# Input products of a decoder trunk as block products of seven multiplications, with attention and pooling put between them

## The chip, the cores and the metric

The kernel runs on one core of one Trainium2 chip. The metric is the device time of the whole program in microseconds (us). Three runs of the kernel before gave a median of 2831.74 us (2831.07 to 2831.84). The profile shows one execution, of 2828.03 us; its span from the first to the last instruction is 2826.3 us. The engines are named as in the profile: PE is TensorE, DVE is VectorE, ACT is ScalarE, POOL is GpSimd, SP is SyncE; PE, DVE, ACT and POOL compute, SP and POOL issue DMAs here.

## What is computed

One pre-norm block on x of 2048 positions by 1024 channels. The normalised input goes through one input projection into queries, keys and values of 12 heads, the pooling input (768 channels) and two gates (1024 channels each). Attention runs over three head groups with windows dilated by 1, 4 and 16 positions; their outputs are combined with weights from their softmax denominators. Pooling takes trailing means over 2, 4, 8 and 16 positions. Both are projected, gated, added, projected again and added to x; a squared-ReLU MLP (1024 to 4096 to 1024) and a last norm follow.

```python
HEAD_DIM = 64
ATT_GROUPS = ((128, 1), (512, 4), (2048, 16))
HEADS_PER_GROUP = 4
POOL_WINDOWS = (2, 4, 8, 16)
D_FF = 4 * D_MODEL
...
    s = jnp.einsum('znqhd,znkhd->znhqk', qb, kb) * (Dh ** -0.5)
    ...
    s = jnp.where(valid[None, :, None], s + bias[None, None], -jnp.inf)
    lse = jax.nn.logsumexp(s, axis=-1)
    p = jnp.exp(s - lse[..., None])
    o = jnp.einsum('znhqk,znkhd->znqhd', p, vb).reshape(Z, Lp, H, Dh)[:, :L]
...
    wts = jax.nn.softmax(jnp.stack(lses, axis=0), axis=0)
    merged = jnp.sum(wts[..., None] * outs, axis=0)
```

## The kernel before

Activations lie with channels on the partitions and positions along the row, in blocks of 128 by 512; a chunk `c` is 512 positions, a half `hf` 1024. Every large product is done to float32 accuracy with three matmuls of rounded parts: an operand is cast to a high part (ACT), the difference to it is the low part (DVE), and high by high, high by low and low by high are summed in PSUM.

The program is one list of stages; a scheduler puts each engine's instructions in order, and they run in that order. The stages are:

- fold: the pooling projection is multiplied by the per-group map into `w_pzg_d` (L213 to L234).
- a1 (the first `for c in range(NCH)`): per chunk, `gained_x` loads x times a gain without the norm, six products give q, k, v of group 2, and the sum of squares becomes `rstd`, which is applied where the results leave PSUM.
- a2: per chunk, six products for the pooling input, the pooling sums (L372), and one block of `attn_g2` after four of the six.
- a3: per chunk, `norm_x`, then q, k, v of groups 1 and 0, `attn_block` for each of four blocks per group (four heads at a time: scores `s` L307, bias L311, maximum L314, exponential L316, transposes `t` L321, copy L323, output `o` L329, copy L331), and the combination of the three groups (L458 to L502), whose weights go to DRAM (`wts_d`) and come back spread over the partitions (`wb`).
- gates(0), merge(0), gates(1), residual(0), merge(1), mlp_in(0), residual(1), mlp_in(1). Gates, residual and mlp_in go through `stage`: a pair of 128-row weight tiles against a half of the input is a 2 by 2 block product done with seven multiplications (`ORDER1`) instead of eight. Two pairs run side by side; each of the seven steps is 12 matmuls of 512 columns per pair. The blocks of the input that all pairs share (`mB11` to `mT4`) are made once per stage.
- the second MLP product, also with seven multiplications, and the last norm.

Only the stages from gates on use seven multiplications; in a1 to a3 each product has its full number of matmuls: 1728 of 512 columns and 1152 of 256 columns (the values, computed with positions on the partitions).

## Time and profile before

| | |
|---|---|
| median of three runs | 2831.74 us |
| profiled execution, and its span | 2828.03 us, 2826.3 us |
| PE busy | 2643.4 us (94%) |
| DVE busy | 1849.3 us (65%) |
| ACT busy | 1337.5 us (47%) |
| POOL busy | 369.6 us (13%) |
| mean granted clock of TensorE | 0.967 |

Busy shares are means over stages with different limits. The table by stretches in the rows further down has one line for each stage: 0 to 33.5 us fold, to 175 a1, to 356 a2, to 757 a3 with products, to 798.5 the attention of the last chunk, to 840.3 the combination of the last chunk, to 1007 gates(0), to 1094.6 merge(0), to 1251 gates(1), to 1338 residual(0), to 1433.3 merge(1), to 2160 mlp_in(0), residual(1), mlp_in(1). A PE that is busy is not PE at its peak, since the ends of matmuls are modelled.

### The profile page before, as it was taken

The page shows a single profiled execution, that of the slowest core. Times are in us where ns is not written, and L with a number is a line of the kernel's source. Part 1 is how long each engine was busy: PE and PEld are TensorE (multiplying, and loading weights), DVE is VectorE, ACT ScalarE, POOL GpSimd, SP SyncE. Part 2 cuts the span into 40 slices and gives each one's busy share as a digit, 9 for nine tenths or more (in the row PEclk, how much of TensorE's full clock was granted, in tenths as well). Part 3 has the DMA queues.
Part 4 walks back from the last instruction along what each step waited for, and adds up shares of the span by engine and source line. Part 5 has one row for each costly group of instructions (what it writes and reads, how often), then busy time and mean ns, then how long its engine had stood idle before and what let it go on. Part 6 is the DMA issues. An engine that isn't in the chain of part 4 may idle for free.

```text
span 2826.3 us, 37148 instructions
## 1 busy us (share of the span) xinstructions
PE 2643.4 (94%) x12966; PEld 2170.3 (77%) x12966; DVE 1849.3 (65%) x2908; ACT 1337.5 (47%) x2472; POOL 369.6 (13%) x581
## 2 busy tenths in 40 slices
...
GB/s 262 75 108 171 167 195 142 151 93 99 79 73 164 117 257 186 111 217 251 231 224 180 161 174 257 212 199 194 189 183 231 257 146 188 229 236 112 137 101 131
DMA packets 213469, 486.67 MB, mean 172 GB/s; under 512 B 37312, under 2 KB 44480, under 8 KB 213152
## 3 DMA queue, kind: packets, MB, share of 16 engines
...
q8 instruction: 102, 1.67, 0.2%
q14 instruction: 87, 0.71, 0.1%
...
## 4 chain that ended last, share of the span: by engine, by line
PE 51%; issue 27%; DMA 10%; DVE 6%; POOL 4%; ACT 2%; SPq 0%; POOLq 0%; DVEq 0%; ACTq 0%
PE z L535 6%; PE z L536 6%; PE z L534 6%; PE z_c_b L534 2%; PE z_c_b L535 2%; PE z_c_b L536 2%; DMA wb<-wts_d 2%; PE mm_v L275 2%; POOL hid_d L734 1%; DMA x<-hid_d 1%; PE z_g_b L535 1%; PE z_g_b L536 1%; PE z_g_b L534 1%; PE mm L127 1%; PE mm L125 1%
## 5 line engine op out<-in xcount | busy, mean ns | idle before, releaser
L528 DVE TENSOR_TENSOR wl_S<-r_S,wh_S 128x512 fp32r<-128x512 f32 x128 | 88.7, 693 | 123.8 <-ACT wh_S L527 123.8
L527 ACT CAST wh_S<-r_S 128x512 fp32r<-128x512 f32 x128 | 79.7, 623 | 176.5 <-PE z L535 154.0
L535 PE MATMUL z<-xl_T,wh_S 128*128 128x512 f32 x384 | 149.6, 390 | 2.8 <-DVE xl_T L528 2.8
L528 DVE TENSOR_TENSOR wl_c_S<-s_c,wh_c_S 128x512 fp32r<-128x512 f32 x128 | 87.0, 690 | 95.5 <-ACT wh_c_S L527 95.3
L536 PE MATMUL z<-xh_T,wl_S 128*128 128x512 f32 x384 | 149.4, 389 | 0.0
L316 ACT ACTIVATE sb_g<-sb_g,negm 128x256 f32<-128x256 f32 (+1 forms) x192 | 86.2, 451 | 119.6 <-DVE negm L314 119.6
L534 PE MATMUL z<-xh_T,wh_S 128*128 128x512 f32 x384 | 138.7, 389 | 0.0
L527 ACT CAST wh_c_S<-s_c 128x512 fp32r<-128x512 f32 x128 | 77.0, 616 | 79.2 <-PE z_c_c L535 43.1
L527 ACT CAST wh_A<-r_A 128x512 fp32r<-128x512 f32 x96 | 59.5, 620 | 104.8 <-PE z L535 63.3
L528 DVE TENSOR_TENSOR wl_A<-r_A,wh_A 128x512 fp32r<-128x512 f32 x96 | 66.1, 690 | 64.8 <-ACT wh_A L527 64.1
L535 PE MATMUL z<-xl_B,wh_A 128*128 128x512 f32 x256 | 102.0, 399 | 1.5 <-DVE xl_B L528 1.5
L126 PE MATMUL mm_a<-xl_a,hi_a 128*128 128x512 f32 x256 | 102.2, 400 | 0.0
L125 PE MATMUL mm_a<-xh_a,hi_a 128*128 128x512 f32 x256 | 100.6, 400 | 1.4 <-ACT qk L410 1.4
L534 PE MATMUL z<-xh_B,wh_A 128*128 128x512 f32 x256 | 95.0, 404 | 7.1 <-ACT xh_B L527 6.6
L127 PE MATMUL mm_a<-xh_a,lo_a 128*128 128x512 f32 x256 | 101.5, 397 | 0.0
L536 PE MATMUL z<-xh_B,wl_A 128*128 128x512 f32 x256 | 99.3, 396 | 0.0
L527 ACT CAST wh_c_A<-r_c 128x512 fp32r<-128x512 f32 x96 | 59.5, 619 | 72.7 <-PE z_c_c L535 28.0
L817 POOL TENSOR_TENSOR y<-y,frs 128x256 f32<-128x256 f32 x4 | 3.2, 811 | 656.9 <-ACT fsq L802 649.3
L535 PEld LDWEIGHTS z<-xl_T,wh_S 128*128 128x128 f32 x384 | 72.1, 188 | 18.6 <-DVE xl_T L528 3.7
L527 ACT CAST wh_g_S<-s_g 128x512 fp32r<-128x512 f32 x64 | 39.4, 620 | 98.8 <-DVE s_g L601 36.0
L528 DVE TENSOR_TENSOR wl_c_A<-r_c,wh_c_A 128x512 fp32r<-128x512 f32 x96 | 65.9, 686 | 29.3 <-ACT wh_c_A L527 29.3
L536 PEld LDWEIGHTS z<-xh_T,wl_S 128*128 128x128 f32 x384 | 72.1, 188 | 14.9
(502 smaller groups left out, 8670.6 us busy)
## 6 DMA issues: line engine op xcount, KB each, us to landing
x<-hid_d SPq DMA_DIRECT2D x160, 256.0 KB, 4.5
...
r_S<-w2s_d SPq DMA_DIRECT2D x128, 256.0 KB, 2.6
x_a<-in_xt SPq DMA_DIRECT2D x96, 256.0 KB, 3.9
r_A<-in_w SPq DMA_DIRECT2D x96, 256.0 KB, 3.5
...
```

What stands on the lines that cost most here:

```text
L125: nc.tensor.matmul(ps, lh, rh, start=(i == 0), stop=False)
L126: nc.tensor.matmul(ps, lh, rl, start=False, stop=False)
L127: nc.tensor.matmul(ps, ll, rh, start=False, stop=(i == n - 1))
L275: nc.tensor.matmul(pv[t][:, :256], a, b, start=(k == 0 and n == 0), stop=(k == KD - 1 and n == 2))
L316: nc.scalar.activation(s[:, h, :W], s[:, h, :W], AF.Exp, bias=negm[:, col + h:col + h + 1], accum_out=l[:, col + h:col + h + 1])
L527: nc.scalar.copy(hi, src)
L528: nc.vector.tensor_sub(lo, src, hi.bitcast(F32))
L534: nc.tensor.matmul(ps, lh, rh, start=start and i == 0, stop=False, skip_group_check=True)
L535: nc.tensor.matmul(ps, lh, rl, start=False, stop=False, skip_group_check=True)
L536: nc.tensor.matmul(ps, ll, rh, start=False, stop=stop and i == n - 1, skip_group_check=True)
L734: nc.gpsimd.dma_start(hid_d[hf][i][j], t)
L817: nc.gpsimd.tensor_mul(y, y, rs)
```

## The change

All products of the normalised input now go through `stage`, one call per half, with 20 pairs: per head group two pairs of q and k and one pair of v, three pairs of the pooling input, eight pairs of gates. Groups go in the order 1, 0, 2 in half 0 and 2, 1, 0 in half 1. The input blocks come from `normed_x` and `combine`: both chunks of the half are loaded, their sums of squares made, and x normalised before the blocks are formed. The results go to DRAM (`qk_d`, `v_d`, `pz_d`, `sg_d`) with the positions of a group's dilation put together; values are transposed by PE in `v_pair` first.

Attention is done in units of two heads (`attention`), 96 of them, and pooling in `pooling`, both called from `hook(j)` after the two pairs of group `j`: five units (half 0) or eight (half 1) after each group from the second on, pooling after groups 6, 7 and 8. After group 8 of half 0 the hook prepares the input of half 1; after group 8 of half 1 it makes the weights of the three head groups for all positions at once (`group_weights`). The combination itself moves into `merge`, and so does the sigmoid of the gates.

In this part PSUM has three banks `b` and two `c` for products, and single banks `s0`, `s1` (scores) and `t`, which the transposes, the output of a unit, the transposed values and the sums of squares share; afterwards four `b` and four `c`. `WB` goes from 5 to 4 and `ZB` from 11 to 10. The stages after it now run as merge(0), merge(1), residual(0), residual(1), mlp_in(0), mlp_in(1). Per half, the input products are 20 pairs of 7 steps of 12 matmuls of 512 columns, 3360 in all. The 96 transposes for the values are new. The second MLP product is unchanged.

```diff
-        for c in range(NCH):
-            cs = slice(c * C, (c + 1) * C)
-            ssq = a1.tile([P, C], F32, name=f"ssq{c}", tag="ssq", bufs=2)
-            u = gained_x(c, f"a1_{c}", ssq, a1)
...
-                mm3_chunk(pqk[i], wqk[i], u)
...
-        for c in range(NCH):
-            u = gained_x(c, f"a2_{c}")
-            for n in range(6):
-                w = split_load(w_pzg_d[n], D, f"wz{c}_{n}", lo_on=nc.gpsimd)
...
-    ORDER1 = ("A11 B11 b", "S1 T1 c", "S2 T2 b", "S4 B22 c", "S3 T3 b", "A12 B21 a", "A22 T4 b")
-    RAWB, SB, WB, ZB = 4, 5, 5, 11
+    ORDER1 = ("A11 B11 b", "S1 T1 c", "S2 T2 b", "S4 B22 c", "S3 T3 b", "A12 B21 c", "A22 T4 b")
+    RAWB, SB, WB, ZB = 4, 5, 4, 10
...
+        for t in range(2):
+            for k in range(KD):
+                tag = {(0, 0): "tt", (1, 0): "hx", (1, 1): "h22", (0, 1): "zz"}[t, k // KH]
+                x = load(k, t, tag)
+                if tag != "zz":
+                    got[k, t] = x
+                if k == 0:
...
+                else:
+                    sq = wtile(f"xsq_{hf}_{k}_{t}")
+                    nc.scalar.square(sq, x)
+                    nc.vector.tensor_add(ssq[t], ssq[t], sq)
+            ps = psd.tile([P, C], F32, name=f"xst_{hf}_{t}", tag="t")
+            ssq_to_rstd(wp, ps, ssq[t], ssq[t], f"x{hf}_{t}", ("zz",) * 3, ZB)
...
+        def piece(k, t, tag):
+            x = got.get((k, t))
+            if x is None:
+                x = load(k, t, tag)
+            nc.vector.scalar_tensor_tensor(x, x, g_mix[:, k:k + 1], ssq[t], op0=ALU.mult, op1=ALU.mult)
...
+                for key, _, scale, onto, fin in js:
+                    wh, wl = split(wp, w[key][a], f"{key}_{a}", "w", WB)
+                    first = n in (0, 1, 5)
                     if first:
-                        bank[j, bk] = ps_c(f"{kj}_{bk}")
-                    ps = bank[j, bk]
+                        bank[key, bk] = bank_of(bk, f"{key}_{bk}{n}")
+                    ps = bank[key, bk]
                     mm_acc(ps, [(wh[:, k * P:(k + 1) * P], wl[:, k * P:(k + 1) * P], *m[b][k])
...
+                        fin(1, 0, ps, None)
+            if hook:
+                hook(j0 // 2)
...
+        def fin(row, t, ps, mid):
+            c = 2 * hf + t
+            o = wtile(f"zq_{key}_{row}_{t}") if mid is None or d > 1 else mid
+            if d > 1:
+                total(o.rearrange("p (r i) -> p r i", r=d), ps.rearrange("p (i r) -> p r i", r=d),
...
+            nc.gpsimd.dma_start(qk_d[g][2 * i + row, :, :, c * C // d:(c + 1) * C // d],
+                                o.rearrange("p (r i) -> p r i", r=d))
...
+        def fin(row, t, ps, mid):
+            z = finished(key, row, t, ps, mid)
+            pt = psd.tile([P, C], F32, name=f"vt_{key}_{row}_{t}", tag="t")
...
+                nc.tensor.transpose(pt[:, b * P:(b + 1) * P], z[:, b * P:(b + 1) * P], ident)
...
+            nc.scalar.copy(vt, pt)
+            nc.gpsimd.dma_start(v_d[g][at(hf, t), row * P:(row + 1) * P].rearrange("(b p) f -> p b f", p=P),
...
+        z = temp(f"pz_{key}", "hx", TW)
+        nc.sync.dma_start(z, pz_d[n, :, c * C:c * C + TW])
...
+            nc.vector.tensor_add(s[rows, 2 * w - 1:], prev[rows, 2 * w - 1:], prev[rows, w - 1:H0 + C - w])
...
+        nc.gpsimd.dma_start(p_d[c, n], pf)
...
+        qk = temp(f"qk_{key}", "hx", 3 * P)
+        q, k = qk[:, :P], qk[:, P:P + W]
+        nc.sync.dma_start(q, qk_d[g][hp, :, r, own])
+        nc.sync.dma_start(k, qk_d[g][2 + hp, :, r, ks])
+        vo = temp(f"vo_{key}", "h22", 3 * P)
...
+        nc.sync.dma_start(v, v_d[g].rearrange("(i r) f -> r i f", r=d)[r, ks, hp * P:(hp + 1) * P]
...
+        ps_s = [psd.tile([P, C], F32, name=f"s{par}_{key}", tag=f"s{par}")[:, :W] for par in range(2)]
+        s = temp(f"sb_{key}", "tt").rearrange("p (h j) -> p h j", h=2)[:, :, :W]
...
+            rows = slice(par * HD, (par + 1) * HD)
+            nc.tensor.matmul(ps_s[par], q[rows], k[rows], start=True, stop=True)
+        for par in range(2):
+            nc.vector.scalar_tensor_tensor(s[:, par], steps[:, 2 * P - W:], SLOPES[HPG * g + 2 * hp + par] * d,
...
+        nc.vector.tensor_reduce(nm, s, axis=AX.X, op=ALU.max, negate=True)
+        for par in range(2):
+            nc.scalar.activation(s[:, par], s[:, par], AF.Exp, bias=nm[:, par:par + 1], accum_out=ls[:, par:par + 1])
...
+        ps_t = psd.tile([P, 2, 2 * P], F32, name=f"t_{key}", tag="t")
...
+                nc.tensor.transpose(ps_t[:, par, b * P:(b + 1) * P], s[:, par, b * P:(b + 1) * P], ident)
+        pt = temp(f"pt_{key}", "tt").rearrange("p (h j) -> p h j", h=2)[:, :, :W]
+        nc.scalar.copy(pt, ps_t[:, :, :W])
+        ps_o = psd.tile([P, C], F32, name=f"o_{key}", tag="t")[:, :P]
+        for b in range(nb):
...
+                nc.tensor.matmul(ps_o[par * HD:(par + 1) * HD, :], v[:, b, par * HD:(par + 1) * HD],
...
+        nc.scalar.copy(o, ps_o)
+        nc.gpsimd.dma_start(o_d[g][hp, :, r, own], o)
...
+        pairs = [p for g in order for p in (qk_pair(hf, g, 0), qk_pair(hf, g, 1), v_pair(hf, g))]
+        pairs += [pz_pair(hf, j) for j in range(3)] + [gate_pair(hf, j) for j in range(KD)]
...
+        queue = [b for g in order for b in work[g]]
+        share = -(-len(queue) // (7 if hf == 0 else 8))
+        def hook(j):
+            if j:
+                for _ in range(min(share, len(queue))):
+                    attention(*queue.pop(0))
+            if j in (6, 7, 8):
+                for n in (2 * j - 12, 2 * j - 11):
+                    for t in range(2):
+                        pooling(2 * hf + t, n)
+            if j == 8:
+                if hf == 0:
+                    next_inputs.append(normed_x(1))
+                else:
+                    group_weights()
+        stage(pairs, next_inputs[hf], hook)
...
+    banks.update(pool=pool_of(pbs, "psb", space=PSUM), b=4, c=4)
...
+                    o = temp(f"o_{c}_{g}_{hp}", "hx")
+                    nc.sync.dma_start(o.rearrange("p (r i) -> p r i", r=d),
...
+                    wb = wtile(f"wb_{c}_{g}_{hp}")
+                    nc.gpsimd.dma_start(wb, bass.AP(tensor=wts_d.tensor, offset=wts_d[g, c, 2 * hp].offset,
...
+                    nc.vector.tensor_mul(view, view, o.rearrange("p (r i) -> p r i", r=d))
```

Three places in the order of the instructions matter for what follows. A row is line, operation, output, inputs and shape; the number at the end of a name tells tiles of one name apart.

The first is DVE at the start of the program. Before, the first rows after the constants make the low parts `xl_a1` of x with its gain, between copies of the folded weights:

```order
L233 COPY pzg0_0_148<-mm1_fold0_0_143 128x384
L189 SCALAR_TENSOR_TENSOR xl_a1_0_0_302<-x_a1_0_0_299,colt_97,xh_a1_0_0_301 128x512
L189 SCALAR_TENSOR_TENSOR xl_a1_0_1_309<-x_a1_0_1_306,colt_97,xh_a1_0_1_308 128x512
L233 COPY pzg0_2_166<-mm1_fold0_2_161 128x384
L197 TENSOR_TENSOR ssq0_298<-ssq0_298,sq_a1_0_1_312 128x512
L189 SCALAR_TENSOR_TENSOR xl_a1_0_2_318<-x_a1_0_2_315,colt_97,xh_a1_0_2_317 128x512
L197 TENSOR_TENSOR ssq0_298<-ssq0_298,sq_a1_0_2_321 128x512
L189 SCALAR_TENSOR_TENSOR xl_a1_0_3_327<-x_a1_0_3_324,colt_97,xh_a1_0_3_326 128x512
L233 COPY pzg0_4_184<-mm1_fold0_4_179 128x384
L119 TENSOR_TENSOR lo_wqk0_372<-raw_wqk0_369,hi_wqk0_371 128x1024
```

Now the low parts `mB11l` of the first block stand behind the sums of squares `xss` of eight x tiles, the norm (L134) and the multiplication of x by it (L285):

```order
L134 TENSOR_TENSOR xss_0_0_303<-y_x0_0_345,t_x0_0_350 128x512
L277 TENSOR_TENSOR xss_0_1_304<-xss_0_1_304,xsq_0_4_1_375 128x512
L285 SCALAR_TENSOR_TENSOR xtt_0_0_0_305<-xtt_0_0_0_305,colt_102,xss_0_0_303 128x512
L285 SCALAR_TENSOR_TENSOR xtt_0_1_0_308<-xtt_0_1_0_308,colt_102,xss_0_0_303 128x512
L285 SCALAR_TENSOR_TENSOR xtt_0_2_0_313<-xtt_0_2_0_313,colt_102,xss_0_0_303 128x512
L285 SCALAR_TENSOR_TENSOR xtt_0_3_0_318<-xtt_0_3_0_318,colt_102,xss_0_0_303 128x512
L277 TENSOR_TENSOR xss_0_1_304<-xss_0_1_304,xsq_0_5_1_380 128x512
L142 TENSOR_TENSOR mB11l_u0_0_431<-xtt_0_0_0_305,mB11h_u0_0_430 128x512
L142 TENSOR_TENSOR mB11l_u0_1_436<-xtt_0_1_0_308,mB11h_u0_1_435 128x512
L142 TENSOR_TENSOR mB11l_u0_2_441<-xtt_0_2_0_313,mB11h_u0_2_440 128x512
L277 TENSOR_TENSOR xss_0_1_304<-xss_0_1_304,xsq_0_6_1_385 128x512
L142 TENSOR_TENSOR mB11l_u0_3_446<-xtt_0_3_0_318,mB11h_u0_3_445 128x512
```

The first low part of the input has moved behind the norm of its chunk, so the first products are behind it too.

The second is DVE where half 0 ends, in its last two pairs of gates (`g0_6`, `g0_7`). Before, in the last two pairs of a gates stage (here `g0_2`, `g0_3` in the middle of gates(0), whose rows are like those of any other group) the low parts of the weights of the steps S2, S4, S3, A12 follow one another:

```order
L528 TENSOR_TENSOR wl_g0_3_S2_7858<-s2_g0_3_7756,wh_g0_3_S2_7857 128x512
L528 TENSOR_TENSOR wl_g0_2_S4_7876<-s4_g0_2_7746,wh_g0_2_S4_7875 128x512
L528 TENSOR_TENSOR wl_g0_3_S4_7895<-s4_g0_3_7758,wh_g0_3_S4_7894 128x512
L528 TENSOR_TENSOR wl_g0_2_S3_7914<-s3_g0_2_7745,wh_g0_2_S3_7913 128x512
L528 TENSOR_TENSOR wl_g0_3_S3_7933<-s3_g0_3_7757,wh_g0_3_S3_7932 128x512
L528 TENSOR_TENSOR wl_g0_2_A12_7952<-r_g0_2_0_7739,wh_g0_2_A12_7951 128x512
L649 TENSOR_TENSOR zS2_g0_2_7855<-z_g0_2_c_7805,zS2_g0_2_7855 128x512
L528 TENSOR_TENSOR wl_g0_3_A12_7972<-r_g0_3_0_7751,wh_g0_3_A12_7971 128x512
L649 TENSOR_TENSOR zS2_g0_3_7873<-z_g0_3_c_7824,zS2_g0_3_7873 128x512
L528 TENSOR_TENSOR wl_g0_2_A22_7992<-r_g0_2_1_7741,wh_g0_2_A22_7991 128x512
```

Now the low parts for step S3 (`wl_g0_6_S3`, `wl_g0_7_S3`) come behind 90 rows that start with the pooling sums (`sum_0_2_1`) right after step S4 and end with the normalised x of half 1 (L285) and its differences (L230). The beginning of this piece:

```order
L142 TENSOR_TENSOR wl_g0_6_S4_4480<-s4_g0_6_4350,wh_g0_6_S4_4479 128x512
L142 TENSOR_TENSOR wl_g0_7_S4_4498<-s4_g0_7_4362,wh_g0_7_S4_4497 128x512
L422 TENSOR_TENSOR sum_0_2_1_3855<-pz_0_2_3853 128x527
L422 TENSOR_TENSOR sum_0_2_2_3857<-sum_0_2_1_3855 128x525
L422 TENSOR_TENSOR sum_1_2_1_3866<-pz_1_2_3864 128x527
L428 SCALAR_TENSOR_TENSOR pf_0_2_3859<-sum_0_2_2_3857,pz_0_2_3853 128x512
```

and its end:

```order
L285 SCALAR_TENSOR_TENSOR xh22_1_4_1_4311<-xh22_1_4_1_4311,colt_102,xss_1_1_4242 128x512
L285 SCALAR_TENSOR_TENSOR xh22_1_5_1_4316<-xh22_1_5_1_4316,colt_102,xss_1_1_4242 128x512
L285 SCALAR_TENSOR_TENSOR xh22_1_6_1_4321<-xh22_1_6_1_4321,colt_102,xss_1_1_4242 128x512
L285 SCALAR_TENSOR_TENSOR xh22_1_7_1_4326<-xh22_1_7_1_4326,colt_102,xss_1_1_4242 128x512
L230 TENSOR_TENSOR xtt_1_0_0_4243<-xhx_1_0_1_4293,xtt_1_0_0_4243 128x512
L230 TENSOR_TENSOR xtt_1_1_0_4246<-xhx_1_1_1_4296,xtt_1_1_0_4246 128x512
L230 TENSOR_TENSOR xtt_1_2_0_4251<-xhx_1_2_1_4301,xtt_1_2_0_4251 128x512
L230 TENSOR_TENSOR xtt_1_3_0_4256<-xhx_1_3_1_4306,xtt_1_3_0_4256 128x512
L142 TENSOR_TENSOR wl_g0_6_S3_4516<-s3_g0_6_4349,wh_g0_6_S3_4515 128x512
L142 TENSOR_TENSOR wl_g0_7_S3_4534<-s3_g0_7_4361,wh_g0_7_S3_4533 128x512
L142 TENSOR_TENSOR mT1l_u1_0_4712<-xtt_1_0_0_4243,mT1h_u1_0_4711 128x512
```

Between steps S4 and S3 of one group now stand 46 rows of pooling, 24 rows of sums of squares and norms, and 20 rows that make blocks of the next half.

The third is PE behind the last product of the input. Before, the last rows of the values of group 0 are followed by scores `s`, transposes `t` and outputs `o` of the four blocks of the last chunk:

```order
L126 MATMUL mm_a3v_3_0_3_6968<-lo_a3v_3_0_1_6884,xh_a3_3_7_6307 128x256
L127 MATMUL mm_a3v_3_0_3_6968<-hi_a3v_3_0_1_6883,xl_a3_3_7_6308 128x256
L307 MATMUL s_g0_3_0_6998<-qk_2_0_2_5830,qk_3_0_0_6774 128x128 x2
L307 MATMUL s_g0_3_0_6998<-qk_3_0_2_6840,qk_3_0_0_6774 128x128 x2
L307 MATMUL s_g0_3_0_6998<-qk_2_0_3_5863,qk_3_0_1_6807 128x128 x2
L307 MATMUL s_g0_3_0_6998<-qk_3_0_3_6873,qk_3_0_1_6807 128x128 x2
L307 MATMUL s_g0_3_1_7038<-qk_3_0_2_6840,qk_3_0_0_6774 128x128 x4
L307 MATMUL s_g0_3_1_7038<-qk_3_0_3_6873,qk_3_0_1_6807 128x128 x4
L321 MATMUL t_g0_3_0_7017<-ident_90,sb_g0_3_0_7007 128x128 x8
L307 MATMUL s_g0_3_2_7078<-qk_3_0_2_6840,qk_3_0_0_6774 128x128 x4
L307 MATMUL s_g0_3_2_7078<-qk_3_0_3_6873,qk_3_0_1_6807 128x128 x4
```

Now the last product row of half 1 (`z_g1_7`) is followed by 19 units without a product row between them: four outputs, three units of group 1 and 16 of group 0, up to the rows of `group_weights` (L488, L495), and only then the first product of merge(0):

```order
L149 MATMUL z_g1_7_b0_9425<-mT4l_u1_3_5028,wh_g1_7_A22_9643 128x512
L150 MATMUL z_g1_7_b0_9425<-mT4h_u1_3_5027,wl_g1_7_A22_9644 128x512
L474 MATMUL o_1_2_3_0_8033<-pt_1_2_3_0_8031,vo_1_2_3_0_8014 64x128 x4
L458 MATMUL s0_1_3_3_0_8074<-qk_1_3_3_0_8069 128x256
L458 MATMUL s1_1_3_3_0_8075<-qk_1_3_3_0_8069 128x256
L468 MATMUL t_1_2_3_1_8055<-ident_95,sb_1_2_3_1_8047 128x128 x4
L458 MATMUL s0_1_3_3_1_8103<-qk_1_3_3_1_8098 128x256
L474 MATMUL o_1_2_3_1_8062<-pt_1_2_3_1_8060,vo_1_2_3_1_8043 64x128 x4
L458 MATMUL s1_1_3_3_1_8104<-qk_1_3_3_1_8098 128x256
L468 MATMUL t_1_3_3_0_8084<-ident_95,sb_1_3_3_0_8076 128x128 x4
L474 MATMUL o_1_3_3_0_8091<-pt_1_3_3_0_8089,vo_1_3_3_0_8072 64x128 x4
L468 MATMUL t_1_3_3_1_8113<-ident_95,sb_1_3_3_1_8105 128x128 x4
```

The first product of merge(0) that takes an attention result (`z_pq`) stands another 125 product rows further on. Of the 77 units before that, 65 have product rows between their `t` and their `o`, 22 mostly; the other 12, of group 2 in half 1, stand in two places (four units and eight) without product rows.

## Rows read from the trace of the kernel before

**Rows 1.** First line of the page.

```profile
span 2826.3 us, 37148 instructions
```

**Rows 2.** Busy time by stretches: from:to, length, busy per engine, granted clock, DMA share, GB/s.

```profile
core 0: us, PE busy (x) PEld busy (x) DVE busy (x) ACT busy (x) POOL busy (x), PEclk, DMA share, GB/s
0.00:33.50 33.50, 24.92 (x128) 23.89 (x129) 20.32 (x38) 17.84 (x28) 12.01 (x23) 1.00 0.97 328
33.50:175.00 141.50, 141.50 (x810) 123.31 (x810) 70.49 (x101) 62.44 (x93) 18.31 (x19) 1.00 0.33 108
175.00:356.00 181.00, 174.58 (x887) 131.48 (x885) 159.53 (x243) 84.22 (x211) 77.52 (x67) 0.98 0.49 161
356.00:757.00 401.00, 373.86 (x2614) 313.03 (x2613) 235.36 (x345) 171.97 (x381) 43.31 (x71) 0.95 0.39 127
757.00:798.50 41.50, 32.59 (x311) 27.31 (x309) 19.30 (x36) 17.61 (x51) 0.57 (x1) 0.84 0.37 121
798.50:840.30 41.80, 0.05 (x2) 0.03 (x1) 21.43 (x23) 3.73 (x6) 5.95 (x8) 0.53 0.17 49
840.30:1007.00 166.70, 159.06 (x673) 127.19 (x674) 104.61 (x166) 84.41 (x150) 15.75 (x30) 0.97 0.48 153
1007.00:1094.60 87.60, 87.24 (x385) 71.94 (x384) 54.56 (x88) 19.96 (x38) 9.09 (x17) 1.00 0.71 227
1094.60:1251.00 156.40, 150.45 (x649) 123.19 (x649) 102.36 (x163) 79.08 (x141) 15.09 (x28) 0.98 0.47 149
1251.00:1338.00 87.00, 83.90 (x362) 68.24 (x361) 70.61 (x116) 47.31 (x84) 18.77 (x35) 0.98 0.76 257
1338.00:1433.30 95.30, 91.36 (x386) 73.91 (x385) 58.51 (x95) 22.60 (x42) 10.32 (x20) 0.96 0.70 234
1433.30:2160.00 726.70, 696.68 (x3026) 572.53 (x3024) 487.15 (x779) 402.74 (x710) 139.78 (x260) 0.98 0.56 194
900.00:1000.00 100.00, 100.00 (x443) 82.81 (x442) 48.28 (x74) 44.56 (x78) 10.25 (x19) 1.00 0.38 127
```

**Rows 3.** Chain of waits, 755 to 845 us: start, us, what.

```profile
773.16 1.12 PE s_g L307 x16
...
787.87 1.09 PE o_g L329 x16
...
788.97 1.04 PE t_g L321 x8
...
793.12 0.44 PE t_g L321 x2
...
807.44 3.35 DVE mn L484
...
812.86 2.53 DMA wts_d<-nm
...
827.60 8.80 DMA wb<-wts_d
```

**Rows 4.** Chain of waits, 100 to 140 us: start, us, what.

```profile
128.15 11.70 PE mm_v L275 x96
```

**Rows 5.** Groups by line and shape, VectorE: line, what, count | busy us, mean ns | idle before.

```profile
L528 DVE TENSOR_TENSOR xl_T<-x,xh_T 128x512 fp32r<-128x512 f32 x96 | 65.8, 686 | 1.3 <-ACT xh_T L527 1.3
...
L372 DVE TENSOR_TENSOR sum<-zext 128x527 f32<-128x527 f32 x24 | 33.9, 1411 | 0.6
...
L158 DVE SCALAR_TENSOR_TENSOR u_a<-x_a,colt,rstd 128x512 f32<-128x512 f32 x32 | 23.5, 749 | 5.4 <-issue 3.2 <-DMA u_d<-u_a 0.9 <-DVE sb_g L311 0.5
...
L372 DVE TENSOR_TENSOR sum<-sum 128x525 f32<-128x525 f32 x16 | 15.0, 940 | 0.1
```

**Rows 6.** Groups by line, 760 to 845 us (columns as in rows 5).

```profile
L323 ACT COPY pt_g<-t_g 128x1024 f32<-128x1024 f32 x5 | 5.0, 1008 | 3.3 <-PE t_g L321 3.3
```

**Rows 7.** DMA issues, 811 to 834 us: count, KB each, us to landing.

```profile
wb<-wts_d POOLq DMA_DIRECT2D x6, 256.0 KB, 8.1
```

**Rows 8.** DMA issues, 0 to 36 us.

```profile
w_pzg_d<-pzg POOLq DMA_DIRECT2D x13, 192.0 KB, 6.1
```

763 lines of the change are left out of this document (308 added, 455 removed).

## The prediction

> **What bounds the kernel now.** I read the stretches first [rows 2], because the change touches only some stages. Between 33.5 and 175 us PE is busy without a pause, and so nearly in every later stage; exceptions are the stretch where pooling and group 2's attention run beside products (181 us), the one with attention of groups 1 and 0 (401 us), the attention of the last chunk (41.5 us) and its combination, in which PE does 0.05 of 41.8 us. So PE is the bound, and the time to be had is PE's work and these pauses.
>
> PE's prices: at full clock 443 matmuls of 512 columns take 100 us [rows 2], 0.2257 us each; 96 of 256 columns take 11.70 us [rows 4], 0.122 each. Attention of one block of four heads with two key blocks takes 1.12 us of scores, 1.04 of transposes (0.13 each) and 1.09 of outputs [rows 3], 3.25 in all; a unit of two heads is then 1.62, and half of that with one key block.
>
> Products of the input cost 1728 x 0.2257 + 1152 x 0.122 + 1344 x 0.2257 (both gates stages) = 834 us. Up to the end of merge(1), without residual(0), the program takes 840.3 + 166.7 + 87.6 + 156.4 + 95.3 = 1346 us [rows 2].
>
> What pauses cost: the a2 stretch has 576 matmuls (130 us) and 16 blocks of four heads with one key block (26 us) for its 181 us, so it loses 25 us, 1.6 per block. The mixed a3 stretch has 4 x 66.8 us of products and 83 us of attention, 350 for 401; of the 51 lost some 22 lie at chunk ends (my reading of PE's gaps), so about 1.0 per block of four heads, 0.5 per unit of two.
>
> **The change, part by part**, as a sum from the start to the end of both merges.
>
> (a) The first group of two pairs. Ahead of the last x tile of the first chunk about 9.95 MB are queued on SP (counted from the order); at the 328 GB/s of the fold [rows 2] that is 30 us, landing at 33. Before, products began there. Now the norm's chain comes first, about 8 us, and then 79 DVE rows up to the last low part of step A22; at 0.69 us [rows 5] 54.5 us, against 37.9 us of PE (168 x 0.2257). DVE sets the end: 33 + 8 + 54.5 + 5.4 for PE's last step is about 101, taken as 103; bounds 95 (loads earlier) and 115 (ACT's casts in series with DVE).
>
> (b) The other 19 groups: 19 x 168 x 0.2257 = 720.
>
> (c) Attention outside the tail: 77 of the 96 units, 35 with two key blocks and 42 with one, 35 x 1.62 + 42 x 0.81 = 91; 96 transposes of values at 0.13 are 12. Together 103.
>
> (d) Where the halves meet. DVE has 90 rows between step S4 and S3 of the last gates. 26 pooling sums at 0.7 (a plain row of the width) to 1.41 and 0.94 [rows 5] are 18 to 29 us; 10 multiply-subtracts about 9; 24 rows for the norm 16; 20 rows of blocks 14.6: 58 to 69. PE has four half-steps of cover, 48 matmuls or 10.8 us. That leaves 47 to 58, and before half of it the loads of x, the squares on ACT and the norm's chain must have come, which I put at some 10 more in part. Taken 62, bounds 45 and 75. If PE had work queued here it would cost nothing; in the order it has none, as the next product row is step S3.
>
> (e) Waits in the mixed stretch. 65 units have about 22 products, 5 us, between transposes and outputs, which hides the copy of a unit (1.01 us for four heads [rows 6]); I price them at 0.4, near a3's 0.5: 26. The 12 units of group 2 without products between cost their chain, about 2.5 us (transposes 0.26, copy 0.5, outputs 0.27, copy out, hand-overs, scores), less the 0.81 already counted: 20. Together 46, 0.6 per unit; bounds 0.4 for all (31) and a2's 1.6 (123).
>
> (f) The tail. 19 units come behind the last product, and the single bank `t` makes them a chain: transposes, copy to SBUF, outputs, copy out, then the next. Four blocks of the last chunk took from 773.16 to 793.56 us [rows 3], 20.4 us or 2.55 per two heads, but with one chain for four heads; so 2.55 is the lower bound and 5.1 the upper. From rows: 0.52 + 0.6 to 1.01 + 0.55 + 0.5 and hand-overs, 3.3 taken: 63 us. Pooling of the last half (about 36 us on DVE) lies among them, 25 of it taken as exposed. Then the weights: DVE's rows with the reciprocal of 3.35 [rows 3] and their transposes 27, weights to DRAM 2.53, back spread out 8.80 [rows 3], 12 multiplications and additions 10, hand-overs 6. Together 142 until the first product that takes attention; bounds 115 and 165. The 125 products of merge(0) ahead of it (28 us) and all attention of the tail lie inside.
>
> (g) The remaining 643 products of the merges, 145 us, and 3 for evictions: 148.
>
> The sum is 103 + 720 + 103 + 62 + 46 + 142 + 148 = 1324 against 1346: 22 us less. PE's work falls by 75 - 12 = 63 us, so two thirds of it are given back at the start, the junction and the tail.
>
> Behind it residual(0), mlp_in(0), residual(1), mlp_in(1) take 87.0 + 726.7 = 813.7 [rows 2] for 3360 matmuls, 758 us: 55 lost. The order is new, residuals and MLP halves side by side, with one weight buffer less and separate banks for `b` and `c`. No row prices this; bounds are 35 less (most waits gone) and 22 more (DVE, 73 us busy per residual before, late in the second residual); I take 10 less. The last stages don't change.
>
> So 32 us less: span 2826.3 [rows 1] - 32 = 2794, profiled execution 2796 (it stands 1.7 above its span), and the median of the three runs stands 3.7 above the profiled one: **2800 us**.
>
> **Rivals.**
>
> A, the forecast: chance 0.5, own range 2768 to 2830 (the bounds of a, d, f and the later stages together).
>
> B, the waits hide better: attention and pooling cost PE's time only. Then (e) is 10 and the tail 125: 53 less, 2747 us, own range 2730 to 2768. For it: 65 units have 5 us of products between their links. Against: a3, with a scheduler's order as well, lost 0.5 per unit. 0.2.
>
> C, on the other side: the single banks make PE wait in the mixed stretch as in a2. Bank `t` is passed from transposes to outputs to the next unit, to the transposed values and to the sums of squares, and each time ACT, whose queue also holds the casts of the next products, must have emptied it; PE, in order, waits at the next row. At 1.6 us for 77 units (e) is 123, 77 more: 2877 us. It decides from 1.0 us per unit (32 more). For it: a2 lost just that per block. Against: a2 had POOL make low parts beside DVE, and 5 us of products lie between. 0.19.
> The Trainium skill, Perfetto Trace Analysis, section Matmuls, says that independent matmul groups should rotate through different PSUM banks, so that emptying one overlaps the next; the change keeps this for products and drops it for `t`. By that rule C would be the outcome, 2877 instead of 2800. The trace before agrees at least with the chain where nothing lies between: 20.4 us for four blocks with 13 us of PE's work [rows 3].
>
> D, the stores of group 2's queries and keys, in pieces of 128 bytes, 2048 per store, 16 stores, become the bound. A strided store of 192 KB took 6.1 us [rows 8], 8.1 for 256 KB by size; if pieces count, as spread loads of 256 KB at 8.1 us [rows 7] may suggest with pieces of four times the length, 33 us each. Then eight stores in half 1 take 264 us where attention of group 2 begins one group (38 us) later, and PE waits some 150: 2950. It decides at about 10 us each. 0.04.
> The Trainium skill, DMA: Bandwidth & Descriptors, Specifications, puts the smallest transfer at line rate at 512 bytes, with a read-modify-write below; no row here shows one.
>
> E, the change doesn't do what it says because DVE becomes the bound: a group needs 28 DVE rows per two pairs (19.3 us) and 7 to 10 us for attention, against 38 us of PE and its attention; only groups with pooling, 12 us more, come near. If all six of them run at DVE's pace, some 6 us longer each, 36 more: 2836. 0.07.
>
> **How the numbers follow.** A measurement of this kernel can tell about 0.2%, 5.7 us, from no change. Faster: A's part below 2826 (0.44) and B (0.20), 0.64. Same: A's upper end 0.06, C and E 0.02 each, 0.10. Slower: C 0.17, E 0.05, D 0.04, 0.26. The range of 2738 to 2870 leaves out the lower part of B, the upper of C and D, some 0.2.
>
> **What would show it.** In the profile after: the first 168 products end near 103 us; PE waits near 50 us for a low part of S3 in the last gates of half 0; between the last product of half 1 and the first `pq` some 140 us with PE busy for under half; the waits of products for `t` and of `t` for ACT some 0.6 us per unit. The forecast is wrong if attention's waits are above 1.0 per unit, if stores of group 2 land after more than 10 us each, or if the two residuals side by side cost over 20 us.

## The result and the profile after

The changed kernel takes 2932.38 us (median of four runs, 2930.1 to 2935.8) against 2831.4 for the kernel before on the same chip: a ratio of 1.0359 [1.0341, 1.0377], so 3.6% slower. The profiled run took 2930.1 us. Its page (first line, PE's total, and PE and the granted clock in 40 slices):

```profile
span 2928.3 us, 35991 instructions
...
PE 2647.8 (90%) x11838; PEld 2098.6 (72%) x11838; DVE 1834.1 (63%) x3031; ACT 1364.7 (47%) x2651; POOL 384.2 (13%) x667
...
PE   4799999289999998687899899989999899999996
...
PEclk7899999599989995788999999999999999999998
```

PE is busy for as long as before (2643.4 us), although its products of the input lost 75 us of work. The mean granted clock fell from 0.967 to 0.933, so part of what was saved is paid again as slower matmuls. Slice 8 and slices 16 to 20 of PE and of the clock show where: the middle of the input products, and the stretch behind them.

Busy time by stretches (columns as in [rows 2]); the stretches are first group; groups 2 to 9; where the halves meet; the rest of half 1; attention behind the last product; weights of the groups; until the first product that takes attention (`pq`); rest of the merges; residuals and first MLP product; last stages:

```profile
core 0: us, PE busy (x) PEld busy (x) DVE busy (x) ACT busy (x) POOL busy (x), PEclk, DMA share, GB/s
61.00:125.00 64.00, 45.69 (x174) 35.77 (x175) 56.09 (x88) 30.73 (x51) 4.28 (x6) 0.79 0.22 70
125.00:500.00 375.00, 368.84 (x1813) 284.94 (x1813) 195.36 (x340) 158.78 (x370) 61.04 (x99) 1.00 0.41 127
515.00:654.00 139.00, 74.30 (x296) 57.30 (x293) 107.93 (x178) 54.58 (x91) 16.18 (x24) 0.75 0.36 116
654.00:1096.00 442.00, 436.97 (x2085) 334.74 (x2084) 210.06 (x385) 189.23 (x481) 68.27 (x117) 0.96 0.38 121
1096.00:1186.00 90.00, 75.39 (x313) 41.52 (x312) 46.98 (x86) 35.79 (x117) 15.06 (x28) 0.56 0.42 131
1186.00:1224.00 38.00, 20.55 (x114) 13.78 (x115) 33.29 (x48) 14.01 (x22) 2.80 (x6) 0.64 0.43 141
1224.00:1260.20 36.20, 23.24 (x90) 18.30 (x89) 15.16 (x24) 7.00 (x13) 10.92 (x15) 0.81 1.06 178
1260.20:1438.70 178.50, 155.19 (x645) 124.65 (x644) 114.69 (x179) 61.50 (x110) 25.89 (x42) 0.92 0.86 241
1438.70:2264.90 826.20, 782.76 (x3361) 638.92 (x3359) 576.55 (x920) 463.80 (x805) 157.95 (x294) 0.97 0.55 193
2264.90:2928.00 663.10, 624.53 (x2754) 513.85 (x2754) 444.94 (x725) 322.42 (x546) 3.17 (x4) 0.97 0.56 178
```

Against [rows 2]: the merges end at 1438.7 where before the same work (without residual(0)) took 1346, 92 more; the next four stages take 826.2 for 813.7; the last stages are 3 shorter. In the two long mixed stretches PE shows hardly a pause, yet it needs more time than the products and attention were priced at. Between 1096 and 1260 it shows three kinds of trouble: busy at a granted clock of 0.56, then half idle, then waiting beside DMA.

The sum of the prediction and what the starts of PE's records give for its terms (the twenty groups of 168 products start at 61.6, 124.1, 164.2, ... 500.0, 604.9, 654.1, ... 1049.5, and the last product at 1095.7):

| term | predicted | measured | difference |
|---|---|---|---|
| (a) first group ends | 103 | 124.1 | +21 |
| (c) and (e), 17 groups: all but the first and the two at the junction | 149 | 173 | +24 |
| (d) junction, groups 10 and 11 (104.9 + 49.2 - 75.8) | 62 | 78 | +16 |
| (f) last product to first `pq` | 142 | 164.5 | +22.5 |
| (g) rest of the merges | 148 | 178.5 | +30.5 |
| four stages behind | 803.7 | 826.2 | +22.5 |
| last stages | 666 | 663 | -3 |

The differences add to 133.5, within 1 us of the distance of 2928.3 from the predicted span of 2794. No one term carries it.

The four stages behind need their parts. Before, mlp_in(0), residual(1) and mlp_in(1) were (residual(0) is in [rows 2]):

```profile
1433.30:1748.00 314.70, 309.62 (x1348) 254.19 (x1346) 212.99 (x341) 179.24 (x318) 55.39 (x103) 0.99 0.55 190
1748.00:1841.80 93.80, 79.42 (x334) 64.58 (x335) 72.99 (x119) 44.05 (x78) 18.30 (x34) 0.93 0.72 244
1841.80:2160.00 318.20, 307.65 (x1345) 253.76 (x1344) 201.17 (x321) 179.45 (x316) 66.09 (x123) 0.98 0.52 185
```

and after, both residuals and then both halves of the first MLP product:

```profile
1438.70:1616.00 177.30, 160.09 (x651) 127.01 (x650) 162.97 (x268) 103.30 (x179) 31.07 (x58) 0.92 0.67 227
1616.00:2264.90 648.90, 622.68 (x2712) 511.91 (x2710) 413.58 (x653) 360.50 (x626) 126.88 (x237) 0.98 0.51 183
```

The residuals take 177.3 us where before they took 87.0 + 93.8 = 180.8; the MLP halves take 648.9 where before they took 314.7 + 318.2 = 632.9.

The start, as pieces of the chain:

```profile
6.77 13.57 PE z_fold L172 x64
...
24.14 8.18 DMA xhx<-in_xt
...
49.48 2.09 PE xst L124 x2
```

The load of x that the chain goes through comes only behind the fold's matmuls, and the sums of squares over partitions (`xst`) only at 49.5 us.

The junction, first as PE's waits from 500 to 600 us (waiting line, releaser, us in total, times, longest), then as pieces of the chain:

```profile
PE xst L124 <- DVE xss L277: 52.2, 2, 37.9
```

```profile
539.08 6.14 DMA p_d<-pf
...
545.66 4.32 DMA xz<-in_xt
...
553.06 2.09 PE xst L124 x2
...
569.40 2.09 PE xst L124 x2
```

The pause is not where the prediction put it. No product starts from 512.7 to 576.0 us, and the next one belongs to step S2, ahead of S4 and S3. PE stands at `xst` for half 1, which comes in PE's order while half 0 still has products to do. It waits for x, and x is late: in the chain a store of pooling (`p_d`, 6.14 us) stands right ahead of its load, and in the kernel the tiles of pooling and those of x take the same rings (`tt`, `hx`, `h22`).

Waits of PE in the mixed stretches, 110 to 515 and 597 to 1096 us, the longest of each:

```profile
PE vt_v L387 <- ACT zv_v L389: 2.8, 4, 0.8
...
PE z_qk_c L150 <- DVE wl_qk_S L142: 5.2, 2, 2.9
```

So the single bank `t` makes PE wait for a few us in 900, not for 1.6 us per unit: rival C did not happen in the way it was described. The starts of PE's records show where the time goes instead. In four places units of attention and transposes of values follow one another without a product between them, and the next product starts only 5.6 us (at 216.8), 9.5 (316.2), 12.4 (741.4) and 25.7 us (850.3) after the last one: 53 us in all, in which PE mostly counts as busy.

Behind the last product: pieces of the chain (ACT's copies of the transposes, then POOL's stores of outputs), four short stretches, PE's and ACT's waits and the DMA issues from 1186 us on.

```profile
1098.44 0.59 ACT pt L470
...
1101.13 0.59 ACT pt L470
...
1104.31 0.59 ACT pt L470
...
1121.70 0.53 POOL o_d L477
...
1126.10 0.54 POOL o_d L477
```

```profile
1096.00:1104.90 8.90, 6.10 (x45) 3.36 (x44) 5.35 (x10) 6.01 (x20) 2.15 (x4) 1.00 0.40 131
1104.90:1114.60 9.70, 6.01 (x21) 3.00 (x22) 8.89 (x16) 1.36 (x6) 2.68 (x5) 0.50 0.68 213
...
1120.00:1130.00 10.00, 10.00 (x42) 5.75 (x42) 3.48 (x7) 4.26 (x16) 1.08 (x2) 0.50 0.34 103
...
1144.90:1155.20 10.30, 5.10 (x21) 2.76 (x21) 9.62 (x18) 1.36 (x5) 2.69 (x5) 0.50 0.66 215
```

```profile
PE z_pp L148 <- ACT wh_p L141: 22.2, 2, 12.5
PE row_s L488 <- DVE rows L498: 12.0, 1, 12.0
...
ACT sp L596 <- DMA sp<-sg_d: 49.3, 21, 11.0
```

```profile
wb<-wts_d POOLq DMA_DIRECT2D x12, 256.0 KB, 16.6
```

The 19 units stand there as predicted. The first, at a granted clock of 1.00, follow one another after 2.7 and 3.2 us. From 1105 us on the clock is 0.50, PE is busy without a pause between 1120 and 1130, and a unit takes 4.4 us. Twice some 10 us pass between two units, around 1110 and 1150; there DVE is busy for nine tenths of the time, mostly with pooling, and the next unit waits for it. Further on ACT waits 49 us for gates to land before it can take their sigmoid, and in its queue the casts `wh_p` that PE needs come behind. The spread load of weights takes 16.6 us where before it took 8.1 [rows 7].

### The profile page after: what moved, and what is told of

Same layout as the page of the kernel before. It is cut to its first block, busy times and chain, and to the rows that moved or that the text cites. A ratio compares the mean times of both kernels' runs of the same rounds, so it can differ in the third digit from the quotient of the medians.

```text
span 2928.3 us, 35991 instructions
## 1 busy us (share of the span) xinstructions
PE 2647.8 (90%) x11838; PEld 2098.6 (72%) x11838; DVE 1834.1 (63%) x3031; ACT 1364.7 (47%) x2651; POOL 384.2 (13%) x667
## 4 chain that ended last, share of the span: by engine, by line
PE 60%; issue 21%; DVE 7%; DMA 6%; POOL 4%; ACT 1%; SPq 0%; POOLq 0%; DVEq 0%; ACTq 0%
PE z L149 6%; PE z L150 6%; PE z L148 6%; PE z_c_b L148 4%; PE z_c_b L150 4%; PE z_c_b L149 4%; PE z_c_c L150 3%; PE z_c_c L149 3%; PE z_c_c L148 3%; DMA x<-hid_d 1%; PE z_qk_b L148 1%; PE z_qk_b L149 1%; PE z_qk_b L150 1%; PE s L458 1%; PE z_qk_c L149 1%
## 5 line engine op out<-in xcount | busy, mean ns | idle before, releaser
L142 DVE TENSOR_TENSOR wl_g_S<-s_g,wh_g_S 128x512 fp32r<-128x512 f32 x64 | 44.2, 692 | 107.0 <-ACT wh_g_S L141 104.4
L464 ACT ACTIVATE sb<-sb,negm 128x256 f32<-128x256 f32 (+1 forms) x192 | 87.3, 458 | 45.0 <-DVE negm L462 44.8
L458 PE MATMUL s<-qk 64*128 64x256 f32 (+1 forms) x384 | 100.3, 442 | 7.9 <-DMA qk<-qk_d 4.7
L477 POOL DMA_DIRECT2D o_d<-vo x96 | 52.0, 542 | 403.2 <-ACT vo L476 402.8
L460 DVE SCALAR_TENSOR_TENSOR sb<-steps,s 128x256 f32<-128x256 f32 (+1 forms) x192 | 62.8, 358 | 54.1 <-PE s L458 54.0
L470 ACT COPY pt<-t 128x512 f32<-128x512 f32 (+1 forms) x96 | 47.4, 493 | 91.9 <-PE t L468 91.9
L745 POOL TENSOR_TENSOR y<-y,frs 128x256 f32<-128x256 f32 x4 | 3.2, 811 | 656.5 <-ACT fsq L730 648.9
```

Source lines behind the costliest of these rows:

```text
L142: nc.vector.tensor_sub(lo, src, hi.bitcast(F32))
L458: nc.tensor.matmul(ps_s[par], q[rows], k[rows], start=True, stop=True)
L460: nc.vector.scalar_tensor_tensor(s[:, par], steps[:, 2 * P - W:], SLOPES[HPG * g + 2 * hp + par] * d, ps_s[par], op0=ALU.mult, op1=ALU.add)
L464: nc.scalar.activation(s[:, par], s[:, par], AF.Exp, bias=nm[:, par:par + 1], accum_out=ls[:, par:par + 1])
L470: nc.scalar.copy(pt, ps_t[:, :, :W])
L477: nc.gpsimd.dma_start(o_d[g][hp, :, r, own], o)
```

## The experiments

Two explanations stood against each other: that attention's place costs the time (its single bank, the units piled up behind the last product, its transitions on PE), and that the other chains do (fold and norm at the start, the norm at the junction, weights and pooling behind the last product). All ratios are to the kernel before on the same chip; medians of one set are compared directly, those of different sets by the ratios.

| run | built on | median us | ratio [95%] |
|---|---|---|---|
| e1_o_bank | changed kernel | 2862.93 | 1.0126 [1.0107, 1.0144] |
| e2_no_att | changed kernel | 2622.75 | 0.9273 [0.9250, 0.9296] |
| e3_no_fold | changed kernel | 2908.13 | 1.0282 [1.0260, 1.0304] |
| e4_norm_early | changed kernel | 2920.79 | 1.0326 [1.0308, 1.0343] |
| e5_fill | e1 | 2852.74 | 1.0075 [1.0058, 1.0091] |
| e6_norm_split | e4 | 2897.76 | 1.0238 [1.0217, 1.0258] |
| e7_both | e5 and e6 | 2848.95 | 1.0062 [1.0045, 1.0079] |
| e8_x_first | e7 | 2838.84 | 1.0036 [1.0023, 1.0049] |
| e9_half_weights | e8 | 2858.25 | 1.0105 [1.0086, 1.0124] |
| e10_fold_late | e9 | 2874.85 | 1.0166 [1.0149, 1.0183] |
| e11_weights_after | e9 | 2864.71 | 1.0144 [1.0129, 1.0159] |
| e12_weights_in_merge | e9 | 2860.07 | 1.0130 [1.0113, 1.0147] |
| e13_no_pool | e11 | 2837.35 | 1.0045 [1.0029, 1.0061] |
| e14_pool_ahead | e12 | 2855.22 | 1.0102 [1.0073, 1.0131] |
| e15_no_gate_load | e8 | 2812.20 | 0.9953 [0.9930, 0.9977] |
| e16_mlp_between | e11 | 2873.78 | 1.0164 [1.0147, 1.0181] |
| e17_old_order | e11 | 2887.32 | 1.0211 [1.0188, 1.0234] |
| e18_pool_in_mlp | e16 | 2844.48 | 1.0047 [1.0033, 1.0061] |

### A bank for the outputs, and attention left out

e1 gives the outputs of a unit a bank of their own, taken from the products' `b`:

```diff
-    banks = {"pool": psd, "b": 3, "c": 2}
+    banks = {"pool": psd, "b": 2, "c": 2}
...
-        ps_o = psd.tile([P, C], F32, name=f"o_{key}", tag="t")[:, :P]
+        ps_o = psd.tile([P, C], F32, name=f"o_{key}", tag="o")[:, :P]
```

> One edit: the output of an attention unit gets a PSUM bank of its own, and the products' b banks go from 3 to 2. Theory 1 (the single bank t paces attention in the order of instructions: one unit in about 44 products, so 20 units pile up behind the last product and pooling slips to the meeting of the halves): in the order now 8 units stand behind the last product and 51 DVE rows instead of 90 at the meeting; 12 units at 4.4 us are 53, 39 rows at about 0.65 are 25, so 60 to 85 us less than the changed kernel, near 2855 us. Theory 2 (the pauses come from the stage that spans a whole half: norm, pooling and group weights, whatever attention does): under 30 us less. Theory 3 (attention stalls products in the mixed stretch, and fewer b banks make it worse): no gain or a loss.

It takes 66 us off by the ratios, the largest step of all. The last product ends at the same time (1095.5), but 8 units stand behind it instead of 19, and they run at full clock; first `pq` at 1191.6 instead of 1260.2. The two stretches of e1 (units; then until first `pq`):

```profile
1095.50:1116.30 20.80, 18.44 (x121) 9.97 (x120) 11.66 (x22) 14.39 (x45) 4.31 (x8) 1.00 0.47 148
1116.30:1191.60 75.30, 42.59 (x208) 31.20 (x205) 49.20 (x72) 21.13 (x34) 13.71 (x20) 0.73 0.71 157
```

That is 2.6 us per unit at a granted clock of 1.00, against 4.4 at 0.50. The bank does not make the unit longer: with the single bank, too, the first units stood 2.7 and 3.2 us apart while the clock was 1.00. So the single bank did its harm through the order of the instructions: in it, 19 units instead of 8 came to stand where nothing runs beside them, and 9 us behind the last product the clock fell. Ahead of the last product nothing is gained: the two groups at the junction take 132.9 us instead of 154.1, the seventeen others, which now hold the units that left the tail, 837.1 instead of 817.6. The Trainium skill, Perfetto Trace Analysis, section Matmuls, asks for independent matmul groups to rotate through different PSUM banks; e1 agrees with it, 66 us for one bank, though not by waits of PE at the bank, which were a few us.

e2 leaves attention out altogether (its statistics are constants, and each unit only stores a block of ones); pooling, weights and merges stay:

> Leaves out the attention units: maxima and denominators are constants and each unit only stores a constant block. Theory 1: the mixed stretches fall to 38 us per group of products (about 115 us less), the tail loses 90 us of units, the meeting of the halves the pooling that attention had pushed there (25 us): about 230 us less than the changed kernel, near 2700 us, and the pause between the last product and the first pq is about 80 us. Theory 2: the pauses stay, so only some 120 us less, near 2810 us.

Attention costs 310 us of the changed kernel up to the end of the merges, where 96 units at the prediction's prices are 91 + 19 x 1.62 = 122 us of PE's work. By milestones: last product 1095.7 to 906.0 (190), last product to first `pq` 164.5 to 26.4 (138), merges 178.5 to 196.1 (-18). The 190 ahead of the last product are 152 in the seventeen groups (817.6 to 665.9), 42 at the junction (154.1 to 111.8) and -4 up to the end of the first group. Two mixed stretches of e2 and the merges:

```profile
128.20:440.60 312.40, 311.80 (x1393) 256.50 (x1392) 182.45 (x293) 108.98 (x191) 49.23 (x77) 1.00 0.44 142
592.00:864.20 272.20, 272.05 (x1220) 224.63 (x1219) 158.88 (x246) 94.69 (x165) 40.24 (x69) 1.00 0.40 135
...
932.40:1128.50 196.10, 171.05 (x707) 136.08 (x706) 121.12 (x189) 63.40 (x114) 25.92 (x42) 0.95 0.83 229
```

Eight groups take 312.4 us, 39 each, near the price of products alone (37.9). The merges are not shorter without attention: what holds them, (g), lies elsewhere.

### The start and the junction

e3 leaves the fold out (the pooling input is multiplied with other weights of the same size, loaded from the input).

> Leaves out the fold of the pooling weights (other weights of the same size are read in their place). If the start is set by the DMAs queued ahead of the x tiles, 3.6 MB less in the queue bring the first product from 61.6 us to about 48 and the end of the first group as much earlier: 10 to 15 us less. If it is set by DVE's chain of norm, blocks and low parts behind the loads, under 5 us less.

The first product comes at 37.4 instead of 61.6, and 22 us go in the whole: the fold's 64 matmuls and its loads stand ahead of the norm in every queue, and nothing hides them. The first group itself is as long as before (63.0 and 62.5 us).

e4 loads x for the norm of half 1 five groups ahead into work tiles, and keeps the rest:

```diff
+            if j == 3 and hf == 0:
+                next_ssq.append(norms(1))
             if j == 8:
                 if hf == 0:
-                    next_inputs.append(normed_x(1))
+                    next_inputs.append(normed_x(1, next_ssq[0]))
```

> One edit: the sums of squares and the norm of half 1 are made from an extra load of x after the fourth group of half 0, so that only its use is left at the meeting of the halves. In the order no burst of more than 7 DVE rows stands among the last gates any more. If the pause of 61 us at the meeting (515 to 597 us) is DVE's burst, it goes, less the normalising of 12 tiles that must still come before the next products: 25 to 45 us less than the changed kernel. If the pause is the waits for x and the chain of the norm, it moves to the fourth group: under 10 us less. It costs 16 loads of x more.

9 us less; the pause moved. The two groups at the junction take 107.3 us instead of 154.1, but the fifth group, which now holds `xst`, takes 90.2 instead of 46.6: from 274.5 to 321.3 us no product starts, while units follow one another without products and PE then waits at `xst` (waits from 298 to 325 us):

```profile
PE xst L124 <- DVE xss L266: 11.8, 1, 11.8
```

In e6 the loads and squares stay at that place and `xst` comes two groups later:

```diff
+            if j == 5 and hf == 0:
+                rstds(1, next_ssq[0])
```

> As the run with the early norm of half 1, but the one matmul per chunk that adds the squares over the partitions (xst) is given out two groups after the loads. If PE stopped because that matmul stands in its queue ahead of products and waits for x, the squares and their sums, the pauses of 12.9 and 5.6 us at 302 to 321 us of that run go, and nothing takes their place: 15 to 20 us less than that run, near 2903 us. If the norm itself is the cost, the time stays at 2921 us.

25 us less than e4, 34 less than the changed kernel by the ratios. The last product of half 0 comes at 563.3 and the first of half 1 at 563.5, and the stretch ahead of it has no gap:

```profile
500.00:563.40 63.40, 63.40 (x292) 51.74 (x291) 53.92 (x96) 20.63 (x37) 12.44 (x23) 1.00 0.56 195
```

So the pause ahead of the last steps of half 0 was PE standing in order at `xst` for data that came late; DVE's 96 rows of this stretch lie beside products. Part of it moved once more: the seventh group, which holds `xst` here, takes 68.0 us instead of 46.4, with units and `xst` for 24 us between two products, and the first group of half 1 takes 54.8 for 49.2.

### Filling, and both together

e5 adds to e1 that the units go out in shares over five and six groups instead of seven and eight, and pooling one group earlier:

```diff
-        share = -(-len(queue) // (7 if hf == 0 else 8))
+        share = -(-len(queue) // (5 if hf == 0 else 6))
...
-            if j in (6, 7, 8):
-                for n in (2 * j - 12, 2 * j - 11):
+            if j in (5, 6, 7):
+                for n in (2 * j - 10, 2 * j - 9):
```

> As the run with a bank of its own for the outputs, and the hooks give out more units per group: 7 in half 0, 11 in half 1, pooling one group earlier. In the order no unit stands behind the last product. Theory 1 (units that pile up make the tail): the 96 us between the last product and the first pq of that run shrink to the 28 us of its 125 products and a little, so 50 to 70 us less than that run, near 2800 us. Theory 2 (the weights of the groups and their way through DRAM make the tail, whenever attention ends): the tail stays at 70 us or more, under 25 us less than that run.

No unit is left behind the last product (last attention 1089.7, last product 1111.4), but 69 us still pass to the first `pq`: 14 us less in all. The units were only the upper of several chains in the tail; the weights, their way through DRAM and the first products of merge(0) need 69 us without them.

e7 joins e5 and e6:

> Both edits: a bank for the outputs and more units per group, and the norm of half 1 early with its matmul two groups later. If the causes are apart, their gains add: 25 to 35 us less than with the bank and the units alone, near 2770 us and below the kernel before. If the early loads of x and squares get in the way of attention in half 0, under 15 us less.

Only 4 us under e5, which is not clear of the noise, where e6 had brought 34 to the changed kernel. The last product comes 20 earlier (1091.3); the tail is 70.6 instead of 69 and the merges 191.5 instead of 179.3. What the junction gave (34 us) was taken back, by the sixth and seventh groups (19 us longer, the seventh with `xst` in it) and by the merges (12).

e8 issues the fold behind the loads of x, in tiles of a ring not yet in use:

```diff
+            if pre and j0 == 0:
+                pre()
             for n, step in enumerate(ORDER1):
...
-        stage(pairs, next_inputs[hf], hook)
+        stage(pairs, next_inputs[hf], hook, None if hf else fold)
```

> As the run with both edits, and the fold goes behind the loads of x and of the first weights, in buffers that the first steps don't use yet; its 64 matmuls stay. Leaving the fold out had brought the first product 24 us forward. If the order of the loads is what holds the start, the first product comes at 45 us or earlier instead of 62 and the program takes 10 to 20 us less than with both edits; if the fold's matmuls, now beside the norm's, take the place of the wait, it is within 6 us of it.

10 us less. The first product is later (81.6, the fold's matmuls stand ahead of it), but the first group ends at 119.8 instead of e7's 124.5. By the last product only 1.5 us of the gain are left, and 5 lie in the merges, so that the start is not shown as the cause of the 10 us. This is the best complete version, and still 0.36% slower than the kernel before.

### The weights behind the last product

e9 computes the weights of each half apart, those of half 0 after group 4 of half 1:

```diff
-    def group_weights():
+    def group_weights(hc):
...
+            if j == 4 and hf:
+                group_weights(0)
```

> As the run with x ahead of the fold, and the weights of the three head groups are made for each half apart: for half 0 after the fifth group of half 1, where group 2's units are done, for half 1 at the end. In the order two units stand behind the last product, and the spread loads of merge(0) stand ahead of the last weights. Theory 2 (the way of the weights through DRAM makes the rest of the tail): the 70 us from the last product to the first pq fall to 30 or less, 35 to 50 us less than that run, near 2795 us and below the kernel before. If merge(0) is held by its own loads of attention results and gates, which are as late as before, under 15 us less.

20 us more. e10 also moves the fold behind four steps of the first group:

> As the run with weights by halves, and the fold's matmuls go to the attention's banks and stand among the first group's products in the order. If PE has room in the first group because DVE sets its pace (54 us of DVE rows for 38 us of products), the 23 us of the fold go into that room: the first product comes near 50 us instead of 82 and the program takes 12 to 25 us less than that run. If the loads of the fold now delay the first weights, it is within 6 us of it or slower.

The first product comes at 49.8, but the first group takes 85.4 us instead of 38.2, and the program is 17 us longer than e9. e11 puts half 1's weights behind merge(0), e12 into the middle of it:

> As the run with weights by halves, and the weights of half 1 are given out behind merge(0), so that their transposes stand behind merge(0)'s products in PE's queue. If that run's loss was PE standing 35 us at these transposes with merge(0) behind them, first pp follows the last product within some 10 us and the program takes 25 to 40 us less than that run, 2820 to 2833 us; merge(1) then waits for its weights up to 20 us. If merge(0) can't begin earlier because its own inputs are late, within 6 us of it.

> As the run before this one, with the weights of half 1 given out in the middle of merge(0). If merge(1) waited there for its weights, that wait is hidden by the second part of merge(0): 8 to 20 us less than the run before this one, near 2810 us. If the buffers that the weights hold slow the loads of the gates in merge(0), no gain or a loss of up to 15 us.

Neither gains on e9. PE's longest wait behind the last product in e9, then PE's and ACT's in e11:

```profile
PE row_s L522 <- DVE rows L532: 34.8, 1, 34.8
```

```profile
PE z_pp L148 <- ACT mB11h_pa L141: 31.4, 1, 31.4
...
ACT mB11h_pa L141 <- DMA p<-p_d: 30.9, 2, 30.4
```

A pause of the same length with another name: once the weights no longer hold PE, the pooling results do, which go to DRAM and back.

e13 (on e11) leaves pooling out: its input is copied to its output, without sums. e14 (on e12) puts pooling ahead of a group's units. e15 (on e8) leaves the gates' loads and sigmoids out of the merges.

> As the run with the weights of half 1 behind merge(0), with the pooling left out: the pooled tiles are copied unpooled from DRAM to DRAM. In that run PE stood 31 us before merge(0) for a low and high part of a pooled tile whose load came late. If pooling (36 of its 48 DVE rows of half 1 stand behind the last product, its tiles wait in rings of four and its stores in POOL's queue) holds that load, the pause falls under 10 us and the program takes 25 to 45 us less than that run, near 2825 us. If the load is held by the buffers of the attention units, the pause stays over 20 us.

> As the run with the weights in the middle of merge(0), and each hook gives out pooling ahead of its attention units. In the order 22 instead of 36 pooling rows of half 1 stand behind the last product, and 10 instead of 4 rows of scores. If pooling is what holds merge(0), 5 to 15 us less than that run; if the units behind the last product hold it just as well, within 6 us or slower.

> As the run with x ahead of the fold, with the gates left out of the merges: no loads of them, no sigmoid. If the 186 us from the first pq to the end of the merges, for 145 us of products, are ACT's queue standing behind sigmoids that wait for their loads, they fall to about 155 and the program takes 25 to 40 us less than that run. If the merges wait for the spread weights and the attention results, under 12 us less.

Without pooling the first `pp` (a product that takes a pooling result) follows 0.2 us behind the last product and the first `pq` 22.6, and 28 us go by the ratios; but the merges then take 226. e14 can't be told from e12. Without gates' loads 0.8% go, some 23 us: 14 between last product and first `pq`, 10 from there to the first product of the residuals, a stretch that was in e8 and is in e15

```profile
1160.00:1346.00 186.00, 156.27 (x644) 124.41 (x643) 116.31 (x181) 62.11 (x111) 25.95 (x42) 0.93 0.87 235
```

```profile
1144.50:1320.20 175.70, 153.92 (x644) 122.59 (x642) 117.46 (x185) 31.37 (x58) 26.43 (x43) 0.94 0.64 172
```

with a DMA share of 0.64 instead of 0.87. So of (g)'s excess a part is the gates' way from DRAM through ACT, and the rest stays.

e16 to e18 (on e11) put other work over the weights and the pooling of half 1: e16 residual(0) ahead of them and mlp_in(0) behind, e17 the order of before (residual(0) between the merges, behind the weights), e18 spreads weights and pooling over the pairs of mlp_in(0).

```diff
+            if hf == 0 and n == 1:
+                group_weights(1)
+            if hf == 0 and 1 <= n <= 6:
+                for t in range(2):
+                    pooling(2 + t, n - 1)
```

> As the run with the weights of half 1 behind merge(0), and the stages run as merge(0), residual(0), weights and pooling of half 1, mlp_in(0), merge(1), residual(1), mlp_in(1). If the tail cost what it did because nothing but itself was queued on PE, merge(0) now waits for no pooling of half 1, and weights and pooling of half 1 lie beside mlp_in(0): first pp within 10 us of the last product, and 30 to 50 us less than the run with the weights behind merge(0), 2815 to 2835 us. If each stage that follows at once on the one that makes its input opens a pause of 10 us or more, half of that gain or none.

> The same with merge(0), weights and pooling of half 1, residual(0), merge(1), mlp_in(0), residual(1), mlp_in(1), the order of the kernel before. Weights and pooling of half 1 lie beside residual(0), where DVE had 73 to 86 us of work for 76 us of products: if DVE binds there, 10 to 30 us slower than the run with mlp_in(0) in between; if the pauses between a stage and its input's maker decide, 10 us faster than it.

> As the run with mlp_in(0) between the merges, and weights and pooling of half 1 are given out by groups inside mlp_in(0), behind the loads of its first inputs. That run moved the pause instead of closing it: 52 us before mlp_in(0), whose inputs wait for the buffers tt, hx and h22 that pooling holds. If the shared rings were the reason, that pause falls under 10 us and the program takes 40 to 55 us less than that run, 2818 to 2834 us, at or just below the kernel before. If pooling beside mlp_in(0) slows its groups by as much (36 us of DVE in six groups that have 26 us of DVE for 38 us of PE), under 15 us less.

e16 is no better than e11 (6 us more, not clear of the noise), and e17 is 14 us slower than e16. In e16 the pause moves once more, to the inputs of mlp_in(0), whose rings `tt`, `hx` and `h22` pooling holds (waits of PE and ACT, 1300 to 1365 us):

```profile
PE z_c_b L148 <- ACT mB11h_c L141: 51.8, 1, 51.8
...
ACT mB11h_c L141 <- DMA tt_c<-hg_d: 43.3, 3, 41.6
```

In e17 it stands ahead of residual(0), 51 us, again at an input that comes from DRAM. In e18 it is gone: 33 us less than e16 by the ratios, and the first `pq` is 20 us behind the last product. Still it ends at 1.0047: from the first product of mlp_in(0) to the last `pp` of merge(1) it takes 447 us instead of e16's 426, and the mixed stretch 1018 instead of e8's 1008.

## Why the prediction was wrong

The forecast was 32 us less and the result is 102 more in span. The frame was right: PE's work fell, and the start, the junction, the tail and the merges gave it back. The steps that failed are the prices of what is given back, which came out 16 to 30 us too low each; the sum said two thirds of the saved work. In four of them the mechanism failed too: (a) put the fold's matmuls at nothing, (d) named the wrong wait, (f) priced the tail at full clock, and (g) had no queue.

- **(a)** 124.1 instead of 103, outside its bounds. The group itself is as long as priced (62.5 us; the forecast had about 62). The step that failed is its start: loads and norm were to end at 41 us, and the first product came at 61.6. The sum had a time for the queued loads and none for the fold's matmuls, behind which x comes in the chain; e3, without the fold, has the first product at 37.4. Whether its loads or its matmuls cost more was not separated.
- **(c), (e)** 173 instead of 149. Units with products beside them cost about what was priced. A unit of two key blocks stands for 1.54 and 0.59 us between two products otherwise 0.2257 apart, 1.68 in all for 1.62; one of one key block for 1.11 and 0.37, 1.03 for 0.81. The 0.4 of waits per unit came as wider starts of the products around them: all that neighbouring products start later than 0.2257 us adds to 25 us (9 in e2). What failed is the price of the places without products: 53 us in four of them, where the sum had 30 for two.
- **(d)** The size was near (78 for 62, bound 75), which is partly luck, as the place was wrong: not low parts of S3 but `xst`, as e4 and e6 show by moving it. Without attention (e2) 36 of the 78 are left; the sum had nothing for attention there.
- **(f)** 164.5 instead of 142. Units and pooling took 89.8 for 88, which is two errors that cancel: a unit took 4.4 us at half clock instead of 3.3, and pooling took about 12 (the two gaps, less a unit each) instead of 25. The weights took 38.4 for 27, and the way through DRAM and the combination 36.3 for 27, with a spread load of 16.6 us where [rows 7] had 8.1. PE was to be busy for under half of the tail and was so for 119 of 164.5 us.
- **(g)** 178.5 instead of 148, the largest miss. The step counted products and evictions, and no queue: ACT's casts stand behind sigmoids that wait for gates, which e15 shows to be worth 10 of the 30 us. The rest is open; it is there without attention as well (196 in e2).
- **The four stages behind** 826.2 instead of 803.7; 826 as well in e1 and e8, so it belongs to their own order. The residuals side by side, which the prediction feared, took 3.5 us less than before. The step that failed is the 10 us less that was taken without a row: the MLP halves took 16 more, 14 of them in the first group of each (58.8 and 50.3 us, before 46.2 and 49.0, for 37.9 of products). No run tested why.

Of the rivals, B is refuted. C names the right place, the single bank, with the wrong mechanism and the wrong stretch; e1 gives 66 us back at it, more than any other edit that keeps the whole computation. In the mixed groups (c) and (e) leave 70 us over (c)'s 103, 0.9 per unit, just under the 1.0 from which C decides. D did not appear: the stores of queries and keys from 640 to 760 us, group 2's among them, landed after 4.7 us in the median, under half of the 10 from which D decides:

```profile
qk_d<-zq_qk POOLq DMA_DIRECT2D x14, 256.0 KB, 4.7
```

E did not either: in the groups with pooling of half 0 (407.8 to 500 us) PE is busy throughout, DVE for 52.9 of 92.2 us.

The Trainium skill, Perfetto Trace Analysis, section Optimization Strategy, says that a kernel with several regimes may gain by interleaving them. This change does that, and here it did not pay: attention as it is placed costs 310 us for 122 us of its own work, 138 of the 310 behind the last product. The experiments point at shared banks, rings and in-order queues; none of them separates the three for all of it. With attention at its own price e2's time would be 2623 + 122 = 2745 us; that is an estimate, and no version here came near it.

Open remain the rest of (g), the first groups of the MLP halves, and the places without products in the mixed stretch: in e8, the best complete version, four of them still take 66 us (28.2 at 802.1 us, 16.4 with `xst` in it, 12.1 and 9.1), and no run put products there. No complete version beat the kernel before.
